# Two feed-forward layers of a diffusion trunk: weight sums and modulation products go to GpSimd

## The chip, the cores and the metric

The kernel runs on one core of one Trainium2 chip. The metric is the device time of one execution in microseconds (us); the engines are TensorE (PE in the profile), VectorE (DVE), ScalarE (ACT), GpSimd (POOL) and SyncE (SP). Each engine runs its own list of instructions in order, and waits on semaphores for the others.

## The reference

The reference is a two-layer diffusion backbone over 256 latent tokens with 256 context tokens before them, width 1024, in float32. Each layer is

```
x = x + mx[2] * 0.5 * swiglu(modulate(x, gain0, mx[0], mx[1]), ffn1_w1, ffn1_w3, ffn1_w2)
x = x + mx[5] * token_mixer(...)
x = x + mx[8] * 0.5 * swiglu(modulate(x, gain2, mx[6], mx[7]), ffn2_w1, ffn2_w3, ffn2_w2)
mx = split(silu(c) @ ada_w[l] + ada_b[l], 9)          # conditioning: 9 vectors of 1024 per layer
swiglu(h, w1, w3, w2) = (silu(h @ w1) * (h @ w3)) @ w2   # hidden width 2816
```

The context tokens go through the same weights with their own conditioning (c_ctx); in layer 1 they drop out after the mixer. The change touches two things in it: how the four feed-forward blocks and the conditioning vectors (one matrix-vector product per layer and stream) are computed.

## The kernel before

Everything is feature-major: a tile holds 128 features by 512 tokens (256 latent, 256 context). A float32 matmul is made of three fp32r ones: each weight tile is loaded raw (512 KB, 128x1024), ScalarE rounds it to a high part (whi), VectorE subtracts that from the raw tile for the low part (wlo), and PE runs wlo, whi, whi against the split activations (lines 216 to 218).

**Stages.** In order of time: start-up and feed-forward 1 of layer 0; the mixer of layer 0; feed-forward 2 of layer 0; feed-forward 1 of layer 1; the mixer of layer 1; feed-forward 2 of layer 1. The two feed-forwards in the middle are the "Strassen" ones (`STRASSEN`): their first half is done by `ff_pairs`, which takes hidden tiles in pairs (pair 1 to 10) and computes the 2x2 block product with 7 block products in place of 8. `product` is one of them: 24 matmuls of 128x256. For a pair, the four raw weight blocks are called W0 to W3, and the seven weights are W0, W1, W2+W3 (n), W0+W2+W3, W0+W2, W3 and W1+W0+W2+W3. In the order of PE a pair p is: W1 ("b21"), W0+n ("n2"), n ("n1"), W0+W2 ("n3"), then already W0 of pair p+1 ("b11"), then W3 ("n4") and the seventh ("b22").

**Sums before.** n and W0+W2 are made by a plain load followed by a second load on GpSimd's queue that adds into the tile (`block(src, plus)`, line 529); W0+n (line 570) and the seventh sum (line 588) are VectorE additions of 128x1024. W0, W2 and W3 are loaded twice or three times a pair: seven loads for four blocks.

**Groups.** After 8, 8 and 6 hidden tiles (`FF_GROUPS`) an out phase multiplies them by w2: for each of 8 output tiles a weight unit and 8 (or 6) times three matmuls of 128x512, and VectorE adds the result to x (line 412).

**Conditioning.** `ada` is a generator: a step loads one 128x1024 block of the conditioning matrix to one of two `araw` buffers (SP queue) and runs one VectorE dot product per stream (`ada_dot`, line 281; the condition vector is spread over all partitions). `hook(n)` pulls steps worth 2n dots after each hidden tile or pair and after each output tile, at the pace in `PACE`. Vectors 2 to 8 of layer 0 and 0 to 2 of layer 1 are made during the first feed-forward, 3 and 4 of layer 1 in the second, 5 to 8 of layer 1 (latent stream only) in the third.

**Order.** PE's list is as the code is written. The lists of all other engines and queues are put in order by a scheduler ahead of time, so an instruction that is written later can stand ahead of one that is written earlier.

Of the kernel before, what the change touches and what calls it, by code (L numbers as in the profile page):

```python
# [20 lines left out]
D = 1024  # L21
KD = 8
# [29 lines left out]
PACE = ((3.2, 1.5), (0.0, 1.0), (0.0, 1.0))  # L52
# [25 lines left out]
class Builder:  # L78
    TAGS = {"sq": ("a", 2, T), "mod": ("a", 2, T), "silu": ("b", 2, T), "th": ("b", 2, T), "on": ("b", 2, T),
            "gg": ("c", 3, T), "PT": ("c", 3, T), "junk": ("c", 3, T), "acc": ("acc", 2, T), "tail": ("b", 2, T), "s1": ("a", 2, T), "sw": ("a", 2, T), "sv": ("kc", 1, T), "su": ("b", 2, T),  # L80
# [203 lines left out]
    def ada(self, l, mods, cond):  # L284
# [3 lines left out]
        for m in mods:  # L288
            ns = (0,) if l == DEPTH - 1 and m > 4 else (0, 1)
            for k in range(KD):  # L290
                raw = self.araw[k % 2]
                nc.sync.dma_start(raw, a["ada"][l, m, k])
                self.ada_dot(l, m, k, raw, cond, ns)
                if k < KD - 1:
                    yield len(ns)
            for s in ns:
                d = M[:, s, m, :]
                nc.vector.tensor_tensor(out=d, in0=d, in1=sm[:, SM_ADAB + m * KD:SM_ADAB + (m + 1) * KD], op=ALU.add)
# [106 lines left out]
    def out_phase(self, getw, acts, l, gm, halves, acc, after, pre, each=None):  # L405
# [13 lines left out]
        nfirst = 2 if gm == 5 or len(halves) == 1 else 0  # L419
# [105 lines left out]
    def block(self, src, plus=None):  # L525
        raw = self.rawp.tile([128, 1024], F32, tag="raw", name="raw")
        self.nc.sync.dma_start(raw, src)
        if plus is not None:
            self.nc.gpsimd.dma_start(raw, plus, accum_op=ALU.add)
# [12 lines left out]
    def ff_pairs(self, l, i, pairs, B):  # L542
# [3 lines left out]
        add = nc.vector.tensor_tensor  # L546
        begun = {}

        def begin(p):
# [5 lines left out]
            begun[p] = r0, q1, s1  # L555

        out = []
        for p in pairs:
            if p not in begun:
                begin(p)  # L560
            r0, q1, s1 = begun.pop(p)
            g1, g2 = (self.pair("g") for _ in range(2))
            r1 = self.block(W[p, 1])
# [19 lines left out]
            r4 = self.block(W[p, 3])  # L583
            self.product(q1, self.cut_weight(r4), B["n4"], False, True)
# [3 lines left out]
            add(out=r1, in0=r1, in1=r0, op=ALU.add)  # L588
# [14 lines left out]
    def ffn(self, l, i, halves, first, acc, after, pre, begun=None, each=None):  # L603
# [22 lines left out]
        for gi, (f0, f1) in enumerate(FF_GROUPS):  # L626
# [16 lines left out]
            w2 = a["w2c"][l, i] if gi == 2 else a["w2a"][l, i, gi]  # L643
            end = gi == len(FF_GROUPS) - 1
# [3 lines left out]
    def startup(self):  # L648
# [82 lines left out]
        self.adaq = itertools.chain(self.ada(0, range(2, NMOD), cond), self.ada(1, range(3), cond))  # L731
# [692 lines left out]
    def build(self):  # L1424
# [8 lines left out]
        for l in range(DEPTH):  # L1433
# [11 lines left out]
            if not last:  # L1445
                self.adaq = self.ada(l + 1, range(3, 5), self.cond(nc.scalar))
# [6 lines left out]
            else:  # L1453
# [3 lines left out]
                self.adaq = self.ada(l + 1, range(5, NMOD), self.cond(nc.scalar))  # L1457
# [58 lines left out]
def _layout(i):  # L1516
# [16 lines left out]
    g["w2c"] = _cols(w2[:, :, 2048:], 128)  # L1533
    w = np.stack([g["w13"][li] for li in STRASSEN])
# [55 lines left out]
```

## Time and profile before

| | |
|---|---|
| median of 3 runs (lowest, highest) | 2303.07 us (2299.65, 2303.67) |
| profiled execution | 2294.51 us, of it span 2292.6 us |
| mean granted PE clock (1 is full speed) | 0.986 |
| busy share of the span | PE 96%, DVE 71%, ACT 46%, POOL 6% |

The span runs from the first to the last instruction, and some 2 us lie around it. Matmuls overlap each other, so the busy share of PE says when it had work, not how fast it went; its waits and its clock in a stage say what the stage lost.

### The profile page before, as it was taken

Reading aid. Unit: us, or ns where it says so; the run is one execution under the profiler, and the core shown is the slowest. Engines: PE = TensorE matmul, PEld = TensorE weight load, DVE = VectorE, ACT = ScalarE, POOL = GpSimd, SP = SyncE. Lnnn points to the kernel's source line nnn. Section 1 sums busy time; section 2 is a strip of 40 time slices with the busy share of each in tenths; the row PEclk is TensorE's granted clock in tenths of the full one; section 3 lists DMA queues with packets and bytes.
Section 4 is the critical chain, followed back from the end, with each engine's and each line's share of the span. In section 5 each row is a group of like instructions: output and inputs, shape, how many; then the busy total and the mean of one; then the engine's idle time right before and its main releaser. Section 6 shows DMA issues by size and latency. Waiting matters only on the chain.

```text
span 2292.6 us, 36217 instructions
## 1 busy us (share of the span) xinstructions
PE 2207.6 (96%) x13578; PEld 1933.6 (84%) x13578; DVE 1621.8 (71%) x3604; ACT 1058.1 (46%) x2617; POOL 131.8 (6%) x166
## 2 busy tenths in 40 slices
PE   9989989999999999999999998989999999999998
PEld 6868777887788877898898998888988889989998
DVE  4899998658645455678875776777567786777665
ACT  4413223437533256444353545335354574565554
POOL 2000000000000000000000000000000000110000
PEclk9999999999999999999999999999999999999999
DMA  8567665331213313436764635885452233435553
GB/s 316 193 220 230 228 209 193 122 101 56 74 54 97 94 61 96 140 93 199 219 174 119 176 79 152 268 248 173 127 176 91 96 111 116 152 117 178 185 184 111
DMA packets 98271, 345.44 MB, mean 151 GB/s; under 512 B 11312, under 2 KB 12208, under 8 KB 98096
## 3 DMA queue, kind: packets, MB, share of 16 engines
q1 hardware_dynamic: 89568, 313.76, 41.6%
q0 software_dynamic: 7808, 27.27, 6.1%
q8 instruction: 107, 1.75, 0.3%
q10 hardware_dynamic: 720, 2.11, 0.3%
q14 instruction: 68, 0.56, 0.1%
HBM read 338.89 MB, written 4.19 MB: 150 GB/s over the span
## 4 chain that ended last, share of the span: by engine, by line
PE 60%; DVE 16%; issue 11%; DMA 11%; ACT 2%; POOL 0%; POOLq 0%; DVEq 0%; SPq 0%; ACTq 0%
PE mm L216 15%; PE mm L217 15%; PE mm L218 14%; DVE junk L281 7%; DMA raw<-in_w13p 5%; DMA araw<-in_ada 5%; DVE wlo L522 2%; DVE wlo L207 2%; PE s L216 2%; PE s L217 2%; PE s L218 2%; PE o L211 2%; PE s L211 2%; PE t L211 2%; PE t L912 1%
## 5 line engine op out<-in xcount | busy, mean ns | idle before, releaser
L206 ACT CAST whi<-raw 128x256 fp32r<-128x256 f32 (+1 forms) x1222 | 437.9, 421 | 391.7 <-PE mm L218 139.1
L207 DVE TENSOR_TENSOR wlo<-raw,whi 128x256 fp32r<-128x256 f32 x1214 | 481.8, 440 | 185.0 <-ACT whi L206 183.1
L216 PE MATMUL mm<-h,wlo 128*128 128x256 f32 (+2 forms) x1272 | 435.4, 342 | 0.4 <-DVE wlo L207 0.4
L218 PE MATMUL mm<-h,whi 128*128 128x256 f32 (+2 forms) x1272 | 426.3, 335 | 0.0
L217 PE MATMUL mm<-h,whi 128*128 128x256 f32 (+2 forms) x1272 | 426.0, 335 | 0.0
L216 PE MATMUL mm<-g,wlo 128*128 128x512 f32 (+1 forms) x758 | 269.5, 355 | 25.0 <-DVE wlo L207 20.1
L281 DVE SCALAR_TENSOR_TENSOR junk<-araw,cond 128x1024 bf16<-128x1024 f32 x224 | 271.6, 1218 | 22.7 <-DMA araw<-in_ada 22.3
L217 PE MATMUL mm<-g,whi 128*128 128x512 f32 (+1 forms) x758 | 266.7, 352 | 3.2 <-DVE g L601 1.7
L216 PEld LDWEIGHTS mm<-h,wlo 128*128 128x128 f32 (+1 forms) x1272 | 241.1, 190 | 33.2 <-issue 9.4
L218 PE MATMUL mm<-g,whi 128*128 128x512 f32 (+1 forms) x758 | 265.9, 351 | 0.0
L218 PEld LDWEIGHTS mm<-h,whi 128*128 128x128 f32 (+1 forms) x1272 | 240.9, 189 | 25.4
L217 PEld LDWEIGHTS mm<-h,whi 128*128 128x128 f32 (+1 forms) x1272 | 241.3, 190 | 22.4 <-issue 0.2
L216 PE MATMUL s<-h,wlo 128*128 128x256 f32 (+1 forms) x848 | 259.0, 305 | 0.0
L217 PE MATMUL s<-h,whi 128*128 128x256 f32 (+1 forms) x848 | 258.6, 305 | 0.0
L218 PE MATMUL s<-h,whi 128*128 128x256 f32 (+1 forms) x848 | 258.5, 305 | 0.0
L521 ACT CAST whi<-raw 128x1024 fp32r<-128x1024 f32 x140 | 145.5, 1047 | 162.3 <-DMA raw<-in_w13p 84.4
L522 DVE TENSOR_TENSOR wlo<-raw,whi 128x1024 fp32r<-128x1024 f32 x140 | 170.1, 1220 | 29.0 <-ACT whi L521 29.0
L216 PEld LDWEIGHTS mm<-g,wlo 128*128 128x128 f32 x758 | 144.1, 190 | 52.0 <-DVE wlo L207 19.9
L216 PE MATMUL mm<-tf,wlo 128*128 128x256 f32 x480 | 144.9, 302 | 35.9 <-DVE wlo L522 28.7
L216 PEld LDWEIGHTS s<-h,wlo 128*128 128x128 f32 x848 | 163.4, 193 | 6.8
L217 PEld LDWEIGHTS s<-h,whi 128*128 128x128 f32 x848 | 163.1, 192 | 6.7
L218 PEld LDWEIGHTS s<-h,whi 128*128 128x128 f32 x848 | 162.9, 192 | 6.7
(296 smaller groups left out, 3851.5 us busy)
## 6 DMA issues: line engine op xcount, KB each, us to landing
araw<-in_ada SPq DMA_DIRECT2D x128, 512.0 KB, 4.1
raw<-in_w13p SPq DMA_DIRECT2D x100, 512.0 KB, 3.5
raw<-in_w SPq DMA_DIRECT2D x90, 512.0 KB, 4.3
raw<-in_win SPq DMA_DIRECT2D x90, 512.0 KB, 3.5
raw<-in_w2a SPq DMA_DIRECT2D x64, 512.0 KB, 4.1
raw<-in_w13p POOLq DMA_DIRECT2D x40, 512.0 KB, 6.1
raw<-in_w2c SPq DMA_DIRECT2D x32, 384.0 KB, 3.1
raw<-in_wbr SPq DMA_DIRECT2D x24, 512.0 KB, 3.5
```

Source lines behind the costliest of these rows:

```text
L206: nc.scalar.copy(hi[:, c], raw[:, c])
L207: eng.tensor_tensor(out=lo[:, c], in0=raw[:, c], in1=hi[:, c].bitcast(F32), op=ALU.subtract)
L211: self.nc.tensor.matmul(out, lhsT=lhsT, rhs=rhs, start=start, stop=stop)
L216: nc.tensor.matmul(out, lhsT=sl, rhs=mh, start=start, stop=False, **kw)
L217: nc.tensor.matmul(out, lhsT=sh, rhs=ml, start=False, stop=False, **kw)
L218: nc.tensor.matmul(out, lhsT=sh, rhs=mh, start=False, stop=stop, **kw)
L281: self.nc.vector.scalar_tensor_tensor(out=junk, in0=raw, scalar=1.0, in1=cond[s], op0=ALU.mult, op1=ALU.mult, accum_out=self.mods[l][:, s, ...
L521: nc.scalar.copy(hi, raw)
L522: nc.vector.tensor_tensor(out=lo, in0=raw, in1=hi.bitcast(F32), op=ALU.subtract)
L912: nc.tensor.transpose(pt[:, b * 128:(b + 1) * 128], P[:, b * 128:(b + 1) * 128], self.ident)
```

## The change

In the two Strassen feed-forwards each weight block is loaded once. All four sums of a pair are GpSimd additions of 128x1024 (`sums`): n when the pair is begun, then n+W0 in place, W2+W0 in place, and W1+n in place. W1 and n live in the pool of activations (`qkv`), the others in the four raw buffers as before.

The conditioning of layer 1 leaves VectorE: a step loads its block on GpSimd's own queue, GpSimd multiplies it by the condition vector in two halves of 128x512 per stream (`ada_product`), and ScalarE adds each half up while copying it in place. Vectors 0 to 3 of layer 1 are made in the second feed-forward, 4 to 8 in the third; the first one keeps only layer 0's seven vectors. `PACE` is changed with it.

Out phases in the two Strassen feed-forwards come after 6, 6, 6 and 4 hidden tiles (`ST_GROUPS`, weights laid out anew in w2s and w2t), that is four in place of three with the same matmuls in all. Where an out phase has 6 hidden tiles, its first two output tiles are now multiplied together, hidden tile by hidden tile (`nfirst`).

```diff
-PACE = ((3.2, 1.5), (0.0, 1.0), (0.0, 1.0))
+PACE = ((2.2, 0.9), (1.5, 0.6), (1.2, 0.6))
+ST_GROUPS = ((0, 6), (6, 12), (12, 18), (18, 22))
...
+    def ada_product(self, l, m, k, raw, cond, streams, part):
+        nc = self.nc
+        for s in streams:
+            for i in range(2):
+                c = slice(i * T, (i + 1) * T)
+                j = self.tmp("prod")
+                nc.gpsimd.tensor_tensor(out=j, in0=raw[:, c], in1=cond[s][:, c], op=ALU.mult)
+                out = part[:, s, k:k + 1] if i else self.mods[l][:, s, m, k:k + 1]
+                nc.scalar.activation(j, j, AF.Copy, accum_out=out)
...
-                nc.sync.dma_start(raw, a["ada"][l, m, k])
-                self.ada_dot(l, m, k, raw, cond, ns)
+                (nc.gpsimd if pool else nc.sync).dma_start(raw, a["ada"][l, m, k])
+                if pool:
+                    self.ada_product(l, m, k, raw, cond, ns, part)
+                else:
+                    self.ada_dot(l, m, k, raw, cond, ns)
...
-        nfirst = 2 if gm == 5 or len(halves) == 1 else 0
+        nfirst = 2 if gm == 5 or len(halves) == 1 or len(acts) == 6 else 0
...
+        sums = nc.gpsimd.tensor_tensor
...
+            r2, r3 = self.block(W[p, 2]), self.block(W[p, 3])
+            n = self.block(None, self.qkv)
+            sums(out=n, in0=r2, in1=r3, op=ALU.add)
+            begun[p] = r0, r2, r3, n, q1, s1
...
-            n = self.block(W[p, 2], W[p, 3])
             wn = self.cut_weight(n)
-            add(out=r0, in0=r0, in1=n, op=ALU.add)
-            self.product(q1, self.cut_weight(r0), B["n2"], False, False)
+            sums(out=n, in0=n, in1=r0, op=ALU.add)
+            self.product(q1, self.cut_weight(n), B["n2"], False, False)
             sv = self.tmp("sv")
             nc.scalar.copy(sv, q1)
+            sums(out=r2, in0=r2, in1=r0, op=ALU.add)
             self.product(q3, wn, B["n1"], True, False)
-            r3 = self.block(W[p, 0], W[p, 2])
-            self.product(q1, self.cut_weight(r3), B["n3"], False, False)
+            sums(out=r1, in0=r1, in1=n, op=ALU.add)
+            self.product(q1, self.cut_weight(r2), B["n3"], False, False)
...
-            r4 = self.block(W[p, 3])
-            self.product(q1, self.cut_weight(r4), B["n4"], False, True)
+            self.product(q1, self.cut_weight(r3), B["n4"], False, True)
...
-            add(out=r1, in0=r1, in1=r0, op=ALU.add)
...
-        self.adaq = itertools.chain(self.ada(0, range(2, NMOD), cond), self.ada(1, range(3), cond))
+        self.adaq = self.ada(0, range(2, NMOD), cond)
...
-                self.adaq = self.ada(l + 1, range(3, 5), self.cond(nc.scalar))
+                self.adaq = self.ada(l + 1, range(4), self.cond(nc.scalar), True)
...
-                self.adaq = self.ada(l + 1, range(5, NMOD), self.cond(nc.scalar))
+                self.adaq = self.ada(l + 1, range(4, NMOD), self.cond(nc.scalar), True)
```

GpSimd's list before, from the reload of x after the mixer of layer 0 to the end of the third feed-forward (line 529 is the adding load, line 333 the power for a norm):

```order
L1388 DMA x<-spill_646 128x512 x8
L529 DMA raw<-in_w13p 128x1024
L333 TENSOR_TENSOR rstd<-ms,neghalf 128x2
L529 DMA raw<-in_w13p 128x1024
L333 TENSOR_TENSOR rstd<-ms,neghalf 128x2
L529 DMA raw<-in_w13p 128x1024 x19
L333 TENSOR_TENSOR rstd<-ms,neghalf 128x2
```

It holds nothing else there: 40 adding loads and the norms.

GpSimd's list in the changed kernel at the same place, from the second sum of pair 1 to the third of pair 2 in the second feed-forward (line 576 is n, 594 is W2+W0, 590 is n+W0, 596 is W1+n; line 290 is a half product, line 303 the load of a conditioning block):

```order
L594 TENSOR_TENSOR raw<-raw 128x1024
L590 TENSOR_TENSOR raw<-raw 128x1024
L596 TENSOR_TENSOR raw<-raw 128x1024
L576 TENSOR_TENSOR raw<-raw 128x1024
L303 DMA araw<-in_ada 128x1024 x2
L594 TENSOR_TENSOR raw<-raw 128x1024
L290 TENSOR_TENSOR prod<-araw,cond 128x512 x4
L303 DMA araw<-in_ada 128x1024
L290 TENSOR_TENSOR prod<-araw,cond 128x512 x4
L303 DMA araw<-in_ada 128x1024
L290 TENSOR_TENSOR prod<-araw,cond 128x512 x4
```

Behind the last of these rows stand a load and then line 590 of pair 2: three conditioning blocks (12 half products) have come to stand between n of pair 2 and n+W0 of pair 2.

The same list at pair 3, up to its line 590 (ahead of these rows, and behind line 594 of pair 3, stand five half products and two loads, then six blocks of four half products and a load each):

```order
L290 TENSOR_TENSOR prod<-araw,cond 128x512 x4
L303 DMA araw<-in_ada 128x1024
L290 TENSOR_TENSOR prod<-araw,cond 128x512 x4
L303 DMA araw<-in_ada 128x1024
L290 TENSOR_TENSOR prod<-araw,cond 128x512 x3
L590 TENSOR_TENSOR raw<-raw 128x1024
L290 TENSOR_TENSOR prod<-araw,cond 128x512
L596 TENSOR_TENSOR raw<-raw 128x1024
```

In all, 40 half products and 10 loads stand between lines 594 and 590 of pair 3, among them products whose hooks are written behind pair 5 and in the second out phase. In the second feed-forward 107 half products, 28 loads and 14 sums stand between n of pair 2 and n+W0 of pair 5 (that included), and the last product of the stage stands ahead of n+W0 of pair 6. In the third feed-forward, where a block has four half products for vector 4 and two for vectors 5 to 8, it is 74 half products, 31 loads and 14 sums to the same place.

VectorE's list before, in the middle of the second feed-forward (line 522 is wlo of a block, 598 and 601 belong to `gated`):

```order
L601 TENSOR_TENSOR g<-sw,g 128x256
L570 TENSOR_TENSOR raw<-raw 128x1024
L522 TENSOR_TENSOR wlo<-raw,whi 128x1024
L588 TENSOR_TENSOR raw<-raw 128x1024
L522 TENSOR_TENSOR wlo<-raw,whi 128x1024
L598 TENSOR_TENSOR su<-su 128x256
L590 TENSOR_TENSOR sv<-sv,s 128x512
L522 TENSOR_TENSOR wlo<-raw,whi 128x1024
```

and in the changed kernel (line 538 is wlo, 617 and 620 are `gated`):

```order
L538 TENSOR_TENSOR wlo<-raw,whi 128x1024 x2
L600 SCALAR_TENSOR_TENSOR sw<-sw,s 128x512
L617 TENSOR_TENSOR sw<-sw 128x256
L620 TENSOR_TENSOR g<-sw,g 128x256
L617 TENSOR_TENSOR su<-su 128x256
L620 TENSOR_TENSOR g<-su,g 128x256
L609 TENSOR_TENSOR sv<-sv,s 128x512
```

The two additions of a pair (570, 588) are gone from it, and no dot (281) stands in this stage's list any more.

## Rows read from the trace of the kernel before

**Rows 1.** Busy time by stage: PE, PEld, DVE, ACT, POOL (instructions), clock, DMA share, GB/s.

```profile
60.00:425.00 365.00, 340.97 (x1522) 277.74 (x1521) 323.31 (x696) 111.03 (x296) 4.86 (x8) 0.99 0.64 212
995.40:1345.00 349.60, 331.74 (x2265) 309.69 (x2265) 251.26 (x429) 162.88 (x303) 17.02 (x20) 0.98 0.60 170
1370.00:1729.00 359.00, 334.10 (x2247) 312.17 (x2246) 251.06 (x424) 160.48 (x299) 19.75 (x26) 0.96 0.63 187
```

**Rows 2.** Groups of VectorE in the first feed-forward, 60 to 425 us.

```profile
L281 DVE SCALAR_TENSOR_TENSOR junk<-araw,cond 128x1024 bf16<-128x1024 f32 x160 | 193.9, 1218 | 9.4 <-DMA araw<-in_ada 9.2
```

**Rows 3.** Groups of VectorE in the second feed-forward, 995.4 to 1345 us.

```profile
L522 DVE TENSOR_TENSOR wlo<-raw,whi 128x1024 fp32r<-128x1024 f32 x68 | 82.5, 1220 | 14.2 <-ACT whi L521 14.2
L281 DVE SCALAR_TENSOR_TENSOR junk<-araw,cond 128x1024 bf16<-128x1024 f32 x32 | 38.7, 1216 | 1.8 <-DMA araw<-in_ada 1.7
L570 DVE TENSOR_TENSOR raw<-raw 128x1024 f32<-128x1024 f32 x9 | 11.0, 1226 | 32.3 <-DMA raw<-in_w13p 32.3
L601 DVE TENSOR_TENSOR g<-sw,g 128x256 fp32r<-128x256 f32 x10 | 4.2, 422 | 3.4 <-ACT g L600 3.4
L598 DVE TENSOR_TENSOR sw<-sw 128x256 f32<-128x256 f32 x10 | 4.2, 418 | 0.0
```

**Rows 4.** Groups of GpSimd in the whole span.

```profile
L529 POOL DMA_DIRECT2D raw<-in_w13p x40 | 34.2, 856 | 690.6 <-DMA raw<-in_w13p 244.0 <-DVE x L412 107.0 <-DVE wlo L522 104.0
L207 POOL TENSOR_TENSOR wlo<-raw,whi 128x768 fp32r<-128x768 f32 x8 | 14.6, 1829 | 21.2 <-ACT whi L206 21.2
L1388 POOL DMA_DIRECT2D x<-spill x16 | 8.8, 550 | 120.2 <-DVE hacc L384 120.2
```

**Rows 5.** GpSimd, one instruction after another: two single-input copies of different width.

```profile
1955.48 0.69 POOL L1220 COPY mqk<-krope 32x512 f32<-32x512 f32 x1
1959.76 0.49 POOL L1220 COPY mqk<-qrope 32x256 f32<-32x256 f32 x1
```

**Rows 6.** Loads over the span: queue, count, KB each, median us from issue to landing.

```profile
raw<-in_w13p SPq DMA_DIRECT2D x100, 512.0 KB, 3.5
raw<-in_w13p POOLq DMA_DIRECT2D x40, 512.0 KB, 6.1
x<-spill POOLq DMA_DIRECT2D x8, 256.0 KB, 3.5
```

**Rows 7.** PE's instructions in time: start us, us, line.

```profile
1001.80 0.28 PE L217 MATMUL mm<-tf,whi 128*128 128x256 f32 x1
1001.92 0.28 PE L218 MATMUL mm<-tf,whi 128*128 128x256 f32 x1
...
1083.70 0.39 PE L218 MATMUL mm<-g,whi 128*128 128x512 f32 x1
1083.93 0.39 PE L216 MATMUL mm<-g,wlo 128*128 128x512 f32 x1
```

**Rows 8.** ScalarE groups, 955 to 1370 us: whi of a block, a 128x512 copy.

```profile
L521 ACT CAST whi<-raw 128x1024 fp32r<-128x1024 f32 x72 | 74.8, 1048 | 78.1 <-DMA raw<-in_w13p 37.6 <-PE mm L218 32.6 <-PE s L218 7.7
L578 ACT COPY sw<-mm 128x512 f32<-128x512 f32 x10 | 5.9, 587 | 15.6 <-PE mm L218 15.6
```

**Rows 9.** VectorE and GpSimd at the same moments: start us, us, line.

```profile
44.62 0.49 DVE L377 SCALAR_TENSOR_TENSOR h<-mod,mods,h 128x256 fp32r<-128x256 f32 x1 [0.19 <-ACT h L376]
45.39 1.82 POOL L207 TENSOR_TENSOR wlo<-raw,whi 128x768 fp32r<-128x768 f32 x1 [3.35 <-ACT whi L206]
45.75 1.74 DVE L377 SCALAR_TENSOR_TENSOR h<-mod,mods,h 128x256 fp32r<-128x256 f32 x1 [0.65 <-ACT h L376]
...
1956.66 3.06 POOL L1220 COPY mqk<-krope 32x512 f32<-32x512 f32 x1
1956.82 2.42 DVE L207 TENSOR_TENSOR wlo<-raw,whi 128x256 fp32r<-128x256 f32 x7
```

More of the change, by code (lines that the diff above doesn't have):

```diff
@@ L1 @@
 import heapq
-import itertools
 import math
@@ L282, in ada_dot, with ada @@
                                                 accum_out=self.mods[l][:, s, m, k:k + 1])
-    def ada(self, l, mods, cond):
+    def ada_product(self, l, m, k, raw, cond, streams, part):
[7 more added lines that the diff above has]
+                nc.scalar.activation(j, j, AF.Copy, accum_out=out)
+    def ada(self, l, mods, cond, pool=False):
         nc, a = self.nc, self.a
@@ L289, in ada @@
             ns = (0,) if l == DEPTH - 1 and m > 4 else (0, 1)
+            part = self.sp.tile([128, 2, KD], F32, tag="part", name="part", bufs=1) if pool else None
             for k in range(KD):
                 raw = self.araw[k % 2]
-                nc.sync.dma_start(raw, a["ada"][l, m, k])
-                self.ada_dot(l, m, k, raw, cond, ns)
+                (nc.gpsimd if pool else nc.sync).dma_start(raw, a["ada"][l, m, k])
[3 more added lines that the diff above has]
+                    self.ada_dot(l, m, k, raw, cond, ns)
                 if k < KD - 1:
@@ L297, in ada @@
                 d = M[:, s, m, :]
+                if pool:
+                    nc.vector.tensor_tensor(out=d, in0=d, in1=part[:, s, :], op=ALU.add)
                 nc.vector.tensor_tensor(out=d, in0=d, in1=sm[:, SM_ADAB + m * KD:SM_ADAB + (m + 1) * KD], op=ALU.add)
@@ L523, in cut_weight, with block @@
         return hi, lo
[L525 to L529, printed above, removed]
+    def block(self, src, pool=None):
+        if pool is None:
+            raw = self.rawp.tile([128, 1024], F32, tag="raw", name="raw")
+        else:
+            raw = pool.tile([128, 1024], F32, tag="pair", name="raw")
+        if src is not None:
+            self.nc.sync.dma_start(raw, src)
         return raw
@@ L554, in begin @@
             nc.scalar.copy(s1, q1)
-            begun[p] = r0, q1, s1
-        out = []
+            r2, r3 = self.block(W[p, 2]), self.block(W[p, 3])
+            n = self.block(None, self.qkv)
+            sums(out=n, in0=r2, in1=r3, op=ALU.add)
+            begun[p] = r0, r2, r3, n, q1, s1
         for p in pairs:
@@ L560, in ff_pairs @@
                 begin(p)
-            r0, q1, s1 = begun.pop(p)
+            r0, r2, r3, n, q1, s1 = begun.pop(p)
             g1, g2 = (self.pair("g") for _ in range(2))
-            r1 = self.block(W[p, 1])
+            r1 = self.block(W[p, 1], self.qkv)
             q2, q3 = self.s_bank(), self.s_bank()
@@ L625, in ffn @@
         h = self.hn
-        for gi, (f0, f1) in enumerate(FF_GROUPS):
+        st = (l, i) in STRASSEN
+        groups = ST_GROUPS if st else FF_GROUPS
+        for gi, (f0, f1) in enumerate(groups):
             gts = start
@@ L642, in ffn @@
             ng = f1 - f0
-            w2 = a["w2c"][l, i] if gi == 2 else a["w2a"][l, i, gi]
-            end = gi == len(FF_GROUPS) - 1
+            end = gi == len(groups) - 1
+            if st:
+                j = STRASSEN.index((l, i))
+                w2 = a["w2t"][j] if end else a["w2s"][j, gi]
+            else:
+                w2 = a["w2c"][l, i] if end else a["w2a"][l, i, gi]
             self.out_phase(lambda c: self.unit(w2[c], ng * 128), gts, l, gm, halves,
@@ L1533, in _layout @@
     g["w2c"] = _cols(w2[:, :, 2048:], 128)
+    w2 = np.stack([w2[li] for li in STRASSEN])
+    g["w2s"] = _cols(w2[:, :2304].reshape(len(STRASSEN), 3, 768, D), 128)
+    g["w2t"] = _cols(w2[:, 2304:], 128)
     w = np.stack([g["w13"][li] for li in STRASSEN])
```

2 lines of the change are left out of this document (1 added, 1 removed).

## The prediction

> **What bounds the kernel now.** I read the busy times by stage first [rows 1]. In each of the three feed-forwards that the change touches, PE is the bound, with little lost: the stage less PE's busy time is 24 us, 18 us and 25 us, and the granted clock of 0.99, 0.98 and 0.96 costs another 4, 7 and 14 us (stage times what is missing to 1). That makes 28, 25 and 39 us, 92 us in all: no change to the other engines can win more here. Next, who is behind these waits. In the first feed-forward VectorE is busy 323 of 365 us, 194 us of it the 160 dots of the conditioning [rows 2]. In the second, VectorE idles 32 us before the addition of line 570 for the adding load of a weight sum [rows 3]; the busy times of the third are alike [rows 1]. GpSimd has next to nothing to do in these stages (17 and 20 us) [rows 1].
>
> **What goes away.** Layer 0's seven vectors need 112 dots, so 48 of the 160 leave the first feed-forward: 48 x 1.22 = 58 us off an engine with 42 us to spare. VectorE then has 265 of 365 us to do and follows PE; I take 24 of the 28 us as won. In each of the other two stages 32 dots (39 us) and some 20 additions (20 x 1.22 = 24 us) leave VectorE, and the second and third loads of a block leave the queues. The added out phase brings 16 additions of 128x256 per stage, at the 0.42 us of such an operation [rows 3] 7 us: they cost nothing as long as the 63 us are gone from VectorE. The paired first output tiles have the same matmuls: nothing.
>
> **What GpSimd gets, and its price.** Before, GpSimd runs one kind of two-operand work on wide tiles: 128x768 in 1.83 us [rows 4]. In proportion, a half product (512) is 1.22 us and a sum (1024) 2.44 us; with a fixed share of 0.3 us, read off two copies of 512 and 256 that take 0.69 and 0.49 us [rows 5], they are 1.32 and 2.34. I take 1.25 and 2.4. A load on GpSimd's queue holds it 0.55 us (reload of x) to 0.86 us (adding load) [rows 4]; I take 0.7. It lands after 3.5 us (256 KB) to 6.1 us (512 KB, adding) [rows 6]; I take 5.
>
> The Trainium skill (GPSIMD Engine Reference, Performance versus the Vector engine) gives 4497 ns for such an addition of 2048 elements, about half VectorE's rate, and advises VectorE for it. An estimate from that page, in proportion, is 1.12 and 2.25 us; by it the lateness worked out next would be about 16 us and 11 us smaller in the two stages. The row of this case stands above it.
>
> **Where the sums come to stand.** What decides is GpSimd's order, not its sum. A block product takes PE 24 x 0.12 = 2.9 us, a pair 20.2 us, an out phase of six 8 x 18 x 0.227 = 32.7 us [rows 7]. Counted from pair 1's first product, PE without a wait comes to n2 of pair 2 at 25.9 us, of pair 3 at 78.8, of pair 4 at 99.0, of pair 5 at 119.1. Each n2 needs n+W0 (line 590) plus its whi and wlo, 1.05 + 1.22 = 2.3 us [rows 3, 8].
>
> On GpSimd, n of pair 2 can be done at about 12 us: W3's buffer is free once W0+W2 of pair 1 is cut (2.9 + 2.3), its load lands 3.5 us later [rows 6], the sum takes 2.4, and semaphores come on top. From there to n+W0 of pair 5 the order has 107 half products (134 us), 14 sums (34 us) and 28 loads (20 us), with some 2 us for the first landing: 190 us. Two buffers hide the other landings, since a block's own work (4 x 1.25 + 0.7 = 5.7 us) is longer than 5. So n2 of pair 5 starts at 12 + 190 + 2.3 = 204 us where 119 was due: **84 us late**. It falls into four waits: 14 us at pair 2, 35 at pair 3 (40 half products stand ahead of its line 590), 18 each at pairs 4 and 5. Then PE has 52.9 us of its own to n2 of pair 6 (six products, an out phase, one product) against 21 half products, four sums and four loads, 39 us: no further wait, and the 84 us stay.
>
> In the third feed-forward it is 74 half products (93 us), 14 sums (34 us), 31 loads (22 us). A one-stream block has only 2 x 1.25 + 0.7 = 3.2 us of work, less than a landing: with two buffers 0.9 us of each of 21 blocks can show, 19 us at most; sums stand among them, I take 10. So 12 + 158 + 2.3 = 172 us for 119: **53 us late**. The rest (22 half products, four sums, nine loads, 43 us) is again under PE's 52.9.
>
> ScalarE gets 128 sums in the second and 96 in the third stage, at the 0.59 us of a 128x512 copy [rows 8] 75 and 56 us on top of 163 and 160: not the bound.
>
> **The two engines against each other.** At 45.75 us a VectorE operation with both inputs in SBUF that otherwise takes 0.49 us takes 1.74 us, until 0.3 us after GpSimd's subtraction ends; at 1956.66 us a GpSimd copy takes 3.06 instead of 0.69 us, through seven VectorE subtractions in a row [rows 9]. So they shut each other out. Such work of VectorE is 7 x 1.22 + 8 x 0.42 = 11.9 us a pair [rows 3], 48 us on the four pairs to n2 of pair 5. Bounds: nothing, where it all falls into GpSimd's load issues and landings (22 and 32 us), or all 48. I take 25 and 15 us. In pairs 6 to 10, with no products left, 4 x 2.4 + 11.9 = 21.5 us stand against PE's 20.2: 1.3 us for some nine pairs, I take 10 (0 to 25).
>
> **The sum.** First feed-forward -24; second 84 + 25, less the 25 us that it loses now, +84; third 53 + 15 - 39 = +29; later pairs +10: +99 us. On the profiled 2294.5 us that is 2394; the median of the runs lies 9 us above the profiled one, so I say 2400.
>
> **Rivals.**
> - *No shutting out to speak of* (22%). GpSimd's products wait for ScalarE to free their buffers, which leaves gaps for VectorE. Then -24 + 59 + 14 + 4 = +53: 2356.
> - *Full shutting out* (16%). Every VectorE operation with two SBUF inputs delays GpSimd by its whole time, as the seven in [rows 9] did: 84 + 48 - 25, 53 + 48 - 39, 25 in the later pairs, less 24: +170, 2473. The Trainium skill (SBUF — State Buffer, Who interferes with whom) states this rule: the read interface is lent for a whole instruction, and the other engine stands still. The rows agree with it for single instructions; none shows two engines that are both busy for long.
> - *GpSimd keeps up, and the kernel gets faster* (9%). The price of a half product decides: 0.1 us of it moves the two stages by 10.7 + 7.4 = 18 us, so from the +53 of the first rival, no loss is left at 1.25 - 0.29 = 0.96 us. At the 0.69 us of the 512-wide copy [rows 5] the stages would be 24 and 13 us late instead of 84 and 53: 53 - 100 = -47, 2256. Against it: that copy has one input, and all eight two-operand rows average 1.83 us for 768 [rows 4].
> - *No change to be told* (3%): a price just at that point.
>
> **How the numbers follow.** The forecast, with half of the shutting out, has 50% (2370 to 2445). A measurement of this kernel tells about 0.2%, 5 us, from no change. Forecast, first and second rival are slower, 88%; faster 9%; same 3%. The range runs from below the first rival (2330) to near the second (2460), and leaves out the faster case and the upper half of the full one.
>
> **What would show it.** In the profile after: GpSimd busy over half of both Strassen stages, 224 half products near 1.25 us and 80 sums near 2.4 us or longer; PE waiting at L216 for wlo of n+W0 (line 538) at pairs 2 to 5, the longest at pair 3 in each stage, and its clock down behind these waits; the second feed-forward near 430 us and the third near 390; VectorE's wlo stretched while GpSimd runs; the first feed-forward with PE's waits under 8 us. The prediction is wrong if half products take under 1 us, if GpSimd's order leaves line 590 on time although they don't, or if ScalarE's sums, and not GpSimd, hold the products up by far more than counted.

## The result and the profile after

The changed kernel takes 2552 us where the kernel before takes 2303: ratio 1.1081 (1.1059 to 1.1103). The direction was right; the loss is 249 us and not the 97 that were forecast, and it lies above the range. To see where it went, I cut both spans at the same landmarks: a stage runs from the first cut of the activation forms (line 493 before, 509 after) to the last addition into x (line 412, 428). First the two stages before, then after (columns as in [rows 1]):

```profile
999.10:1346.70 347.60, 329.74 (x2248) 307.66 (x2247) 249.54 (x430) 160.79 (x301) 17.02 (x20) 0.98 0.61 171
1374.50:1733.60 359.10, 334.20 (x2245) 312.14 (x2245) 251.02 (x430) 158.57 (x300) 20.57 (x27) 0.96 0.64 188
```

```profile
967.40:1478.70 511.30, 371.49 (x2232) 338.55 (x2232) 345.80 (x339) 243.59 (x514) 295.95 (x199) 0.85 0.31 102
1510.40:1982.80 472.40, 357.78 (x2231) 326.76 (x2231) 309.68 (x332) 221.28 (x451) 252.64 (x183) 0.87 0.36 119
```

All that lies ahead of the second feed-forward is 31.7 us shorter (999.1 to 967.4): the first feed-forward is rid of its waits. The second is 163.7 us longer and the third 113.3; between them it is 3.9, behind them 10.2. Of the 277 us of the two stages, 212 are idle time of PE (stage less busy: 17.9 and 24.9 us before, 139.8 and 114.6 after), and 65 are slower matmuls: as many instructions keep PE busy 41.8 and 23.6 us longer, at a granted clock of 0.85 and 0.87 between the levels of 1.2 and 2.4 GHz.

No engine is full. GpSimd's 296 us are not the loss by themselves: what stands out is VectorE, which runs 91 instructions fewer than before in the second stage and is busy 96 us longer. Its groups from 967.4 to 1300 us of the changed kernel (busy time and mean ns behind the bar):

```profile
L538 DVE TENSOR_TENSOR wlo<-raw,whi 128x1024 fp32r<-128x1024 f32 x38 | 67.4, 1792 | 23.7 <-ACT whi L537 23.7
L617 DVE TENSOR_TENSOR sw<-sw 128x256 f32<-128x256 f32 x5 | 25.4, 5082 | 3.6 <-ACT sw L616 3.6
L620 DVE TENSOR_TENSOR g<-sw,g 128x256 fp32r<-128x256 f32 x5 | 13.8, 2757 | 2.4 <-ACT g L619 2.4
L428 DVE SCALAR_TENSOR_TENSOR x<-mm,mods,x 128x256 f32<-128x256 f32 x32 | 13.8, 476 | 4.9 <-PE mm L218 4.9
L600 DVE SCALAR_TENSOR_TENSOR sw<-sw,s 128x512 f32<-128x512 f32 x5 | 3.4, 686 | 7.2 <-ACT sw L599 7.2
```

Against [rows 3]: the split of a block takes 1792 ns for 1220, the product of line 617 takes 5082 for 418. The two groups that take one operand from PSUM, the additions into x and line 600, keep their time. Before, from 999.1 to 1346.7 us, they are:

```profile
L412 DVE SCALAR_TENSOR_TENSOR x<-mm,mods,x 128x256 f32<-128x256 f32 x48 | 21.2, 478 | 30.4 <-PE mm L218 30.3
L579 DVE SCALAR_TENSOR_TENSOR sw<-sw,s 128x512 f32<-128x512 f32 x10 | 6.9, 686 | 6.7 <-ACT sw L578 6.7
```

And GpSimd's half products over the whole span are little longer than the 1.25 us that I took:

```profile
L290 POOL TENSOR_TENSOR prod<-araw,cond 128x512 f32<-128x512 f32 x224 | 309.7, 1406 | 56.4 <-ACT prod L292 39.1
```

So the shutting out (one of the two engines standing still beside the other) falls on VectorE. One place shows how it reaches PE: the timeline of four engines at the end of pair 5 (start us, us; in brackets the wait ahead, and for whom).

```profile
1237.19 4.74 DVE L207 TENSOR_TENSOR wlo<-raw,whi 128x768 fp32r<-128x768 f32 x1
1241.86 6.41 DVE L617 TENSOR_TENSOR sw<-sw 128x256 f32<-128x256 f32 x1
...
1236.11 5.00 POOL L290 TENSOR_TENSOR prod<-araw,cond 128x512 f32<-128x512 f32 x4
...
1242.02 2.42 POOL L576 TENSOR_TENSOR raw<-raw 128x1024 f32<-128x1024 f32 x1
1244.39 1.29 POOL L290 TENSOR_TENSOR prod<-araw,cond 128x512 f32<-128x512 f32 x1
1245.64 2.33 POOL L594 TENSOR_TENSOR raw<-raw 128x1024 f32<-128x1024 f32 x1
...
1248.30 0.41 ACT L619 CAST g<-sw 128x256 fp32r<-128x256 f32 x1 [8.89 <-DVE sw L617]
...
1250.33 0.82 ACT L206 CAST whi<-raw 128x768 fp32r<-128x768 f32 x1
...
1251.17 2.02 DVE L207 TENSOR_TENSOR wlo<-raw,whi 128x768 fp32r<-128x768 f32 x1 [2.01 <-ACT whi L206]
...
1253.34 0.76 PE L216 MATMUL mm<-g,wlo 128*128 128x512 f32 x1 [7.73 <-DVE wlo L207]
```

VectorE's 0.42 us product ends 0.3 us after GpSimd's third instruction in a row (1245.64 + 2.33). ScalarE waits 8.89 us for it, the cast of the next weight unit stands behind in ScalarE's order, then VectorE's split, and PE waits 7.73 us. The largest of PE's waits from 967.4 to 1478.7 us (us, times, longest), 119 of some 140 us, all name a split of VectorE. Not every one was followed back to a held instruction:

```profile
PE s L216 <- DVE wlo L538: 43.4, 4, 12.1
PE mm L216 <- DVE wlo L538: 39.4, 9, 10.9
PE mm L216 <- DVE wlo L207: 36.1, 10, 7.7
```

### The profile page after: what moved, and what is told of

Read it like the earlier page. It is cut to its first block, busy times and chain, and to the rows that moved or that the text cites. A ratio compares the mean times of both kernels' runs of the same rounds, so it can differ in the third digit from the quotient of the medians.

```text
span 2552.0 us, 36430 instructions
## 1 busy us (share of the span) xinstructions
PE 2267.9 (89%) x13542; PEld 1981.3 (78%) x13542; DVE 1719.1 (67%) x3306; ACT 1203.6 (47%) x2985; POOL 648.5 (25%) x502
## 4 chain that ended last, share of the span: by engine, by line
PE 56%; issue 18%; POOL 11%; DVE 7%; DMA 4%; ACT 4%; POOLq 0%; SPq 0%; DVEq 0%; ACTq 0%
PE mm L216 14%; PE mm L217 13%; PE mm L218 13%; POOL prod L290 6%; PE s L216 3%; PE s L217 3%; PE s L218 3%; DVE wlo L538 2%; PE o L211 2%; PE s L211 2%; DMA raw<-in_w2s 2%; POOL raw L590 2%; DMA araw<-in_ada 2%; DVE wlo L207 1%; DVE sw L617 1%
## 5 line engine op out<-in xcount | busy, mean ns | idle before, releaser
L207 DVE TENSOR_TENSOR wlo<-raw,whi 128x256 fp32r<-128x256 f32 (+2 forms) x1134 | 504.5, 489 | 292.8 <-ACT whi L206 290.7
L206 ACT CAST whi<-raw 128x256 fp32r<-128x256 f32 (+2 forms) x1142 | 432.0, 439 | 388.0 <-issue 117.3
L216 PE MATMUL mm<-h,wlo 128*128 128x256 f32 (+2 forms) x1272 | 435.6, 342 | 0.0
L216 PE MATMUL mm<-g,wlo 128*128 128x512 f32 (+1 forms) x746 | 277.1, 371 | 72.0 <-DVE wlo L207 50.9
L216 PE MATMUL s<-h,wlo 128*128 128x256 f32 (+1 forms) x848 | 267.1, 315 | 73.6 <-DVE wlo L538 73.3
L290 POOL TENSOR_TENSOR prod<-araw,cond 128x512 f32<-128x512 f32 x224 | 309.7, 1406 | 56.4 <-ACT prod L292 39.1
L538 DVE TENSOR_TENSOR wlo<-raw,whi 128x1024 fp32r<-128x1024 f32 x140 | 246.3, 1773 | 104.5 <-ACT whi L537 104.5
L217 PE MATMUL mm<-g,whi 128*128 128x512 f32 (+1 forms) x746 | 273.5, 367 | 6.5 <-DVE g L620 6.5
L218 PE MATMUL mm<-g,whi 128*128 128x512 f32 (+1 forms) x746 | 271.7, 364 | 0.0
L216 PEld LDWEIGHTS mm<-h,wlo 128*128 128x128 f32 (+1 forms) x1272 | 241.3, 190 | 32.5 <-issue 9.4
L217 PE MATMUL s<-h,whi 128*128 128x256 f32 (+1 forms) x848 | 265.5, 313 | 0.0
L218 PE MATMUL s<-h,whi 128*128 128x256 f32 (+1 forms) x848 | 265.1, 313 | 0.0
L216 PE MATMUL mm<-tf,wlo 128*128 128x256 f32 x480 | 153.7, 320 | 104.3 <-DVE wlo L538 88.6
L216 PEld LDWEIGHTS s<-h,wlo 128*128 128x128 f32 x848 | 170.3, 201 | 82.2 <-DVE wlo L538 44.7
L216 PEld LDWEIGHTS mm<-g,wlo 128*128 128x128 f32 x746 | 147.1, 197 | 103.3 <-issue 48.3
L216 PEld LDWEIGHTS mm<-tf,wlo 128*128 128x128 f32 x480 | 106.6, 222 | 109.6 <-DVE wlo L538 92.6
L292 ACT ACTIVATE prod<-prod 128x512 f32<-128x512 f32 x224 | 140.6, 628 | 106.7 <-POOL prod L290 99.1
```

Of the source, the lines that this page charges most:

```text
L206: nc.scalar.copy(hi[:, c], raw[:, c])
L207: eng.tensor_tensor(out=lo[:, c], in0=raw[:, c], in1=hi[:, c].bitcast(F32), op=ALU.subtract)
L216: nc.tensor.matmul(out, lhsT=sl, rhs=mh, start=start, stop=False, **kw)
L217: nc.tensor.matmul(out, lhsT=sh, rhs=ml, start=False, stop=False, **kw)
L218: nc.tensor.matmul(out, lhsT=sh, rhs=mh, start=False, stop=stop, **kw)
L290: nc.gpsimd.tensor_tensor(out=j, in0=raw[:, c], in1=cond[s][:, c], op=ALU.mult)
```

## The experiments

My theory at first was the prediction's own, Q: the products queued ahead of line 590 make the lateness. The rival, S: the two engines shut each other out. The first four runs take the change apart. Each run's edit is shown in part; `...` or a bracket stands for the rest.

**e1, the sums alone on GpSimd.**

```diff
-                self.adaq = self.ada(l + 1, range(4), self.cond(nc.scalar), True)
+                self.adaq = self.ada(l + 1, range(4), self.cond(nc.scalar))
```

(and the same in the third stage, vectors 4 to 8)

> The changed kernel, but layer 1's conditioning is done as before, by dots on VectorE with loads on SP's queue, at the new pace; GpSimd keeps the weight sums, and the groups of six stay. Theory Q (the products queued ahead of line 590 made the lateness, and all that followed from it): without products GpSimd has 4 x 2.45 = 9.8 us a pair against PE's 20.2, so both stages return to about their length before (348 and 359 us), the first feed-forward keeps its 28 us: 2265 to 2300. Rival S (the two engines shutting each other out is enough by itself): 9.8 us of GpSimd, 11.9 of VectorE and some 4 of dots make 25.5 us a pair, 5 late on each of 20 pairs: 2350 to 2400.

2408 us, 1.0463 (1.0430 to 1.0496): above S's range even, with no product on GpSimd.

**e2, the products alone on GpSimd.**

```diff
-        sums = nc.gpsimd.tensor_tensor
+        sums = nc.vector.tensor_tensor
```

> The changed kernel, but the four weight sums of a pair are done by VectorE; the products stay on GpSimd. No block waits for GpSimd any more, GpSimd only competes with VectorE for operands. Theory Q: VectorE has about 250 - 39 + 7 + 24 = 242 us to do in 348, so the stages end near their length before: 2270 to 2310. Rival S: the products' 224 x 1.25 us are lost to VectorE's two-operand work, 160 and 120 us in the two stages on 242: 400 and 360 us, 50 us late in the second and little in the third: 2320 to 2360. If the raw buffers held across the out phase and not GpSimd make the lateness, it stays here too: over 2400.

2502 us, 1.0867 (1.0829 to 1.0905). That is far above S's range too, and lies in the range that was set for the raw buffers (e8 prices these). No block waits for GpSimd here, and four fifths of the loss stay. Nothing stands queued ahead of line 590 any more, so Q does not carry it. The place itself shows it, n+W0 of pair 5 in the changed kernel, then in e2:

```profile
1213.06 2.55 POOL L590 TENSOR_TENSOR raw<-raw 128x1024 f32<-128x1024 f32 x1
```
```profile
1204.48 1.21 DVE L590 TENSOR_TENSOR raw<-raw 128x1024 f32<-128x1024 f32 x1
```

Counted from the stage's first cut (967.4 and 964.4 us) it begins at 245.7 us behind GpSimd's queue, and at 240.1 where VectorE makes it.

**e3, GpSimd in program order.**

```diff
-            with tc.manual_schedule(engines={ET.PE}):
+            with tc.manual_schedule(engines={ET.PE, ET.Pool}):
```

(and each block's load issued one block ahead)

> The changed kernel with the same work on every engine, but GpSimd's instructions in the order in which the program writes them (8 to 24 half products between the sums of two pairs, each block loaded one block ahead), in place of the order with 107 half products between n of pair 2 and n+W0 of pair 5. Theory Q: a pair costs GpSimd at most 9.8 + 7.5 + 1.2 = 18.5 us, under PE's 20.2, an out phase 33 for 32.7: 2270 to 2330. Rival S: 18.5 + 11.9 = 30 us a pair, 10 late on each of 16 pairs, and some 7 on each of three out phases: 2430 to 2480, no better by much than the change itself.

2518 us, 1.0935 (1.0903 to 1.0967): above S's range as well. The order is worth 35 us of 249, net of what the new order costs. Q falls. GpSimd now waits itself, in the second stage:

```profile
POOL raw L596 <- DVE wlo L544: 97.7, 10, 20.0
POOL raw L582 <- DMA raw<-in_w13p: 43.9, 9, 5.2
```

**e4, the kernel before with the dots moved.**

```diff
-        self.adaq = itertools.chain(self.ada(0, range(2, NMOD), cond), self.ada(1, range(3), cond))
+        self.adaq = self.ada(0, range(2, NMOD), cond)
-PACE = ((3.2, 1.5), (0.0, 1.0), (0.0, 1.0))
+PACE = ((2.2, 0.9), (1.5, 0.6), (1.2, 0.6))
...
```

(and vectors 0 to 3 in the second stage, 4 to 8 in the third, still as dots)

> The kernel before with one thing of the change alone: the first feed-forward keeps layer 0's seven vectors, layer 1's nine are spread over the second and third at the new pace, all as dots on VectorE with loads on SP's queue. Theory: the first feed-forward gains 28 to 32 us; VectorE goes to about 289 of 348 and 275 of 359 us in the others, so they lose little: 2268 to 2285, a gain of 0.8 to 1.5%. Rival: VectorE at 83% is late for weight splits again and again, as it was in the first feed-forward at 323 of 365 us: each of the two stages loses 10 to 15 us more, and the gain is gone, 2290 to 2305.

2310 us, 1.0036 (1.0022 to 1.0050): the rival, 5 us above its range. The first feed-forward gains 33.4 us (999.1 to 965.7), and the two stages give back 25.7 and 23.5, with VectorE at 77% and 70%:

```profile
965.70:1339.00 373.30, 337.40 (x2248) 312.89 (x2247) 285.65 (x502) 162.00 (x301) 17.02 (x20) 0.95 0.61 182
1366.80:1749.40 382.60, 339.21 (x2246) 316.62 (x2245) 269.71 (x467) 158.90 (x300) 20.57 (x27) 0.93 0.62 187
```

Work on an engine that is not full costs time here, among the pairs as I took it (e12 below does not bear that part out). So I formed a third theory, L: a pair is a loop (load, sum, split, sum, split) through one set of buffers, with little slack against PE's 20.2 us; and a rival B, the raw buffers that a begun pair holds across an out phase.

**e5, the sums on VectorE as well** (e1 with e2's edit).

> The run with the sums alone, but the sums too are done by VectorE: GpSimd has nothing of the change, while the groups of six, the order of the sums and the raw buffers stay. Theory L (a pair is a loop of load, sum, split, sum, split through one set of buffers, and GpSimd's 2.4 to 3.3 us a sum makes it longer than PE's 20.2 us): with 1.22 us a sum the loop is 5 us shorter, and VectorE, at 320 of some 350 us a stage, is late as in the first feed-forward: 2320 to 2350. Rival B (the raw buffers held across an out phase and the extra out phase): nothing of that has changed, so it stays near the 2408 of the sums alone, 2385 to 2415.

2356 us, 1.0239 (1.0211 to 1.0268), just above L's range. So 52 us of e1 come from the sums being on GpSimd.

**e6, the groups of six alone** (e4 with ST_GROUPS and the out phases cut to it).

> The kernel before with the dots moved, and the groups of six tiles besides (two more out phases, w2 cut in rows of six, the first two output tiles of a group begun together); sums and loads as before. It tells what the groups cost by themselves. Theory: 16 additions of 128x256 a stage and no more, 2309 to 2320. Rival B in part: more out phases are more places where loads of weights come late; each of two costs some 8 us, 2325 to 2345.

2324 us, 1.0096 (1.0070 to 1.0122): 14 us, between the two.

**e7, no conditioning of layer 1.**

```diff
-                self.adaq = self.ada(l + 1, range(4), self.cond(nc.scalar), True)
+                nc.vector.memset(self.mods[l + 1], 0.5)
+                nc.vector.memset(self.gs[l + 1], 1.0)
```

> The changed kernel with the conditioning of layer 1 left out altogether (its nine vectors are constants, so neither products, nor loads, nor ScalarE's sums): GpSimd has the 80 sums alone, VectorE no dots. Theory L: a pair's loop by itself is 24 to 26 us, as pairs 7 to 10 of the changed kernel show it with no products left, so some 4 us are lost on each of 20 pairs and 5 on each of four out phases: 2330 to 2375, little less than the sums beside VectorE's dots (2408). Rival S (it is the products and dots beside the sums that made the lateness): no wait is left, 2260 to 2285.

2332 us, 1.0134 (1.0106 to 1.0162), in L's range at its lower end. The sums on GpSimd are bearable as long as nothing else competes. Its stages also show VectorE with only the conditioning gone:

```profile
967.10:1348.10 381.00, 340.03 (x2232) 316.23 (x2232) 248.61 (x317) 158.66 (x256) 102.32 (x39) 0.94 0.27 90
1379.60:1761.40 381.80, 340.28 (x2231) 316.16 (x2232) 250.13 (x315) 158.59 (x259) 105.34 (x47) 0.94 0.28 92
```

In the changed kernel VectorE is busy 97 and 60 us longer than here, with 22 and 17 instructions more, nearly all of them 128x8 wide. But e7 is not VectorE's own work: GpSimd's sums stretch it already. Its splits in the second stage:

```profile
L538 DVE TENSOR_TENSOR wlo<-raw,whi 128x1024 fp32r<-128x1024 f32 x70 | 117.4, 1686 | 48.9 <-ACT whi L537 48.8
```

In e14 below, with next to nothing on GpSimd (0.7 and 5.1 us), they take 1222 ns, and VectorE is busy 246 and 245 us with the 40 sums of a stage (49 us) in it; without them it would be 197 and 196. So GpSimd's sums alone stretch VectorE by some 51 and 54 us a stage in e7, and in the changed kernel the whole stretch is some 145 and 110 us. In e7 the stretch gives back what the sums took off VectorE, and the run is 18 us slower than e14.

**e8, W2 and W3 loaded behind the out phase** (on e1).

```diff
+                if p % 3 != 2:
+                    early = load(p + 1)
...
+            r2, r3, n = early or load(p)
```

> The run with the sums alone (2408), but W2 and W3 of the pair behind an out phase are loaded after that phase's weights, not before them, so three raw buffers and not one are left to the out phase. Rival B: the six out phases that waited for w2s loads (64 us of ScalarE's waits in the second stage) run at PE's pace: 30 to 40 us won, 2365 to 2380. Theory L: the phase is faster, but the pair behind it starts its loop from nothing and gives that back: 2395 to 2420.

2378 us, 1.0341 (1.0309 to 1.0373): B is right for 30 us on e1. The line of ScalarE's waits in the second stage of e1, which has no counterpart among the largest of e8:

```profile
ACT whi L206 <- DMA raw<-in_w2s: 64.5, 20, 5.3
```

The other 144 us, from e1 to the changed kernel, are the products on GpSimd and ScalarE's sums of them. The next runs part these two; all but e16 have the weight sums on VectorE, as e2.

**e10, sums without products; e9, products without sums.**

```diff
-                nc.gpsimd.tensor_tensor(out=j, in0=raw[:, c], in1=cond[s][:, c], op=ALU.mult)
-                nc.scalar.activation(j, j, AF.Copy, accum_out=out)
+                nc.scalar.activation(j, raw[:, c], AF.Copy, accum_out=out)
```

(this is e10; e9 keeps the product and leaves out ScalarE's sum, with constants for the vectors)

> The other half of the same pair: ScalarE keeps its 224 sums, over the loaded block as it is, and GpSimd's products are left out (the nine vectors are then not the reference's). Theory S: with no GpSimd beside it VectorE is back at its own times, and ScalarE has 240 of some 380 us: 2310 to 2350. Rival A: ScalarE's own 64 to 75 us a stage in an engine that issues in order are what costs, 2400 to 2480.

2357 us, 1.0242 (1.0216 to 1.0267): S, or a little over it. VectorE's splits of 128x1024 take 1.22 us again. ScalarE's sums wait for the loaded blocks here, 34.8 us in 36 pieces.

> The run with the products alone (2502; the weight sums are VectorE's), with ScalarE's 224 sums of the products left out (the nine vectors are constants): GpSimd multiplies and nobody waits for it. Theory S (GpSimd's products shut VectorE out of its operands; in that run its splits of 128x1024 took 1.79 us in place of 1.22 and its busy time in the second stage was some 100 us over that work's own): the stages stay long, 2450 to 2500. Rival A (ScalarE, which issues in order, stands at a sum until GpSimd's product is done, 42 us in 56 waits in the second stage, and the casts behind it come late): the time falls to that of the run with all of it on VectorE or below, 2310 to 2360.

2484 us, 1.0796 (1.0769 to 1.0823), far from rival A. But the trace spoils the verdict: a reload of the conditioning vector on ScalarE's queue waits for the last product and holds ScalarE for 93.8 us at one go.

**e13 to e16** were to mend this.

> The run with products and without ScalarE's sums once more, but the conditioning vector is reloaded at the first product of the third feed-forward and not at the end of the second, so that no load on ScalarE's queue waits for GpSimd. Theory S: VectorE is held out as before and only the one hold of 94 us goes: 2380 to 2400. If the hold had hidden other lateness: 2420 to 2480.

2488 us, 1.0811 (1.0795 to 1.0827), above both ranges: the reload was issued as early as before, and the hold is 92.1 us.

> The base of the others: weight sums on VectorE, layer 1's conditioning left out altogether. VectorE has 241 us to do in some 350: 2300 to 2330, a little under the same with GpSimd's sums (2332).

2314 us, 1.0060 (1.0043 to 1.0077), as expected.

> The run with the products alone (2502): GpSimd makes the same products and ScalarE as many sums of the same width, but it sums the loaded block and not the product (the nine vectors are not the reference's), so neither waits for the other. Theory C (what costs most is the chain ScalarE's cast behind a sum behind a product that VectorE holds up): only the shutting out and ScalarE's own time are left, 2395 to 2440. Rival: the two loads as such cost, coupled or not: 2480 to 2510.

> The changed kernel with that one coupling taken away in the same manner; sums and products stay on GpSimd, in its own order. Theory C: 2440 to 2490 in place of 2552. Rival: 2530 to 2560.

2528 us, 1.0987 (1.0970 to 1.1003), and 2569 us, 1.1163 (1.1145 to 1.1180): more than with the real products and above all four ranges. They did not uncouple anything: ScalarE's sums wait for the loaded block instead (143 us in e15), and GpSimd issues those loads behind its products. Inconclusive.

**e17, products that nobody waits for; e18, ScalarE's sums over the conditioning vector.**

```diff
+                kept = self.cond(nc.scalar)
...
-                self.adaq = self.ada(l + 1, range(4, NMOD), self.cond(nc.scalar), True)
+                self.adaq = self.ada(l + 1, range(4, NMOD), kept, True)
```

(both; e17 leaves out ScalarE's sums as e9 does, e18 takes them over `cond` in place of the product)

> Weight sums on VectorE, products on GpSimd, ScalarE's sums left out (the nine vectors are constants), and the conditioning vector loaded once for both stages: no engine waits for GpSimd. What is left against the base of 2314 is the shutting out alone. Theory C (shutting out is the smaller part, waits for GpSimd in ScalarE's queue the larger): 2365 to 2400, the 92 us of the hold gone. Theory S: 2440 to 2490.

> The same with ScalarE's 224 sums of the same width put back, over the conditioning vector (the nine vectors are not the reference's), so they wait for nothing. Against the 2502 of the real products this has the same work on every engine without ScalarE's waits for GpSimd. Theory C: 2390 to 2440. Theory S: 2470 to 2510.

2473 us, 1.0759 (1.0743 to 1.0775), and 2477 us, 1.0763 (1.0744 to 1.0783): both in S's ranges by their totals. But e18 does not price ScalarE's sums. They wait for nothing, so the scheduler put them early: 83 of the 224 run ahead of the second feed-forward, and none in the third:

```profile
L292 ACT ACTIVATE aj<-cond x224: 612/631/634, 868.7 to 1184.0; 128x512 bf16<-128x512 f32 x112
```

And both runs still have one hold in the second stage: VectorE's sum n (line 574 in e17) writes a buffer that the last product must have read (52 us in e18; e17's waits of VectorE):

```profile
DVE raw L574 <- POOL prod L290: 65.9, 1, 65.9
```

Their third stages have none (PE's longest wait there is 12.6 us), so the third stages are what to compare: e14 (neither), e10 (ScalarE's sums), e17 (GpSimd's products), e18 (the same, since no sum of ScalarE is left in it), e2 (both, with their waits):

```profile
1370.10:1745.40 375.30, 338.08 (x2236) 315.39 (x2236) 244.91 (x355) 158.96 (x261) 5.10 (x9) 0.94 0.28 94
```
```profile
1383.00:1787.80 404.80, 347.31 (x2236) 320.96 (x2235) 247.75 (x372) 218.05 (x453) 26.21 (x49) 0.93 0.41 139
```
```profile
1479.70:1902.80 423.10, 350.14 (x2236) 322.10 (x2235) 303.07 (x355) 159.11 (x261) 178.01 (x145) 0.91 0.39 133
```
```profile
1483.60:1911.00 427.40, 348.88 (x2237) 321.09 (x2236) 309.52 (x356) 159.54 (x263) 179.13 (x145) 0.91 0.39 132
```
```profile
1482.10:1932.70 450.60, 360.54 (x2235) 330.58 (x2234) 305.59 (x371) 221.64 (x453) 168.40 (x145) 0.89 0.37 125
```

Products alone +48 us (e18 +52), ScalarE's sums +30, both +75: nearly the sum of the two. Each has something else in it: ScalarE waits 24.8 us for loaded blocks in e10 and 45.7 us for products in e2, and all but e14 load the conditioning blocks (ScalarE's waits for w2s are 77.6 us in e17 for 67.1 in e14). The products run nothing on VectorE, and its busy time rises from 245 to 303 us with the same 355 instructions. That is the shutting out in VectorE's time; what it costs is the 48 us, less what the loads may have in them, which no run parts. In the second stage it is e14 378, e10 389, e17 485 less a PE wait of 68.7 that ends the hold, some 416, and e2 488: products +39, sums +11, and 60 us more when the sums wait for real products (in e2 ScalarE waits for line 290 42 us in 56 pieces there). That last 60, the largest of the three, is a difference; no run shows it by itself.

**e11 and e12, one vector moved in the kernel before.**

```diff
-        ... self.ada(1, range(3), cond))
+        ... self.ada(1, range(2), cond))
...
-PACE = ((3.2, 1.5), (0.0, 1.0), (0.0, 1.0))
+PACE = ((2.9, 1.35), (0.0, 1.5), (0.0, 1.0))
```

(e12: 0.8, 1.0 in the second stage; both make vectors 2 to 4 there)

> The kernel before, with one vector (16 dots) moved from the first feed-forward to the second, where all 48 dots stand in the two out phases that have hooks and none among the pairs. Theory (dots cost where they stand among a pair's products, 64 and 48 dots among pairs having made the two stages 26 and 24 us longer; an out phase has room): the first feed-forward wins some 10 us, the second loses 2 to 5: 2294 to 2300. Rival (VectorE then has 1.22 + 0.96 + 3 x 1.22 = 5.8 us for an output tile that takes PE 5.4, so the out phases are late): 2302 to 2308.

> The same vector moved, but 16 of the 48 dots stand among the pairs, about 1.6 for each, and 32 in the out phases as before. If dots among the pairs are what costs, the 16 cost some 0.6 us each, 10 us, and nothing is won: 2300 to 2308. If not, as much is won as in the run before or more: 2292 to 2298.

0.9963 (0.9949 to 0.9978) and 0.9969 (0.9953 to 0.9986): both a little faster than the kernel before, 2294 and 2293 us. e11 has the gain and the loss that were expected: 11.9 us won ahead of the second feed-forward (987.2 for 999.1), and that stage 357.9 for 347.6 us, 10 lost, more than the 2 to 5; its profiled span is thus no shorter by more than 0.6 us, and the interval of the timed runs is what says faster. In e12 it is 14.5 us won (984.6) and 14.1 lost (361.7). Where the dots stand makes no difference that shows, so e11's theory, that dots among the pairs are what costs, is not borne out.

## Why the prediction was wrong

**What fell.** The step "What decides is GpSimd's order, not its sum". The order is as written there, but putting it right wins 35 us (e3), and with no sum on GpSimd at all 2502 of 2552 us stay (e2). In size the lateness at pair 5 of the second stage is not far off: n+W0 begins at 245.7 us of the stage where e14, without conditioning, has it at 141.7, 104 us late for 84 and 25 of shutting out. That is luck: with nothing queued ahead of it, e2 is as late there (240.1). With products that nobody waits for it is 173.0 (e17), with ScalarE's sums over loaded blocks 154.9 (e10); the rest shows in e2, where ScalarE's sums wait for the products as well. So what carries GpSimd's work to PE is, as far as the runs show it, not the queue ahead of line 590 but VectorE's held instructions and ScalarE's list.

**The term that failed with it.** Shutting out was added to GpSimd's queue, 25 and 15 us, as VectorE's work that delays GpSimd. It is mostly the other way round: GpSimd's half products lose 0.16 us each (1.41 for 1.25), 36 us in all, and VectorE loses some 145 and 110 us, 51 and 54 of them to the sums by themselves (e7). VectorE is followed by ScalarE and PE in a pair's loop, where a late split can be a wait; e17 prices the products' part at some 39 and 48 us, loads included, with no other engine's work waiting for GpSimd but for the one hold. The rival of full shutting out had the right engine pair and the wrong victim, and at 2473 was still 79 us short.

**Costed at nothing.** ScalarE was "not the bound" at 75 and 56 us of sums; it is busy 85 and 63 us longer than in e7. The sums cost 43 us in time (e14 to e10), their waits for the loads included, for ScalarE's casts stand behind them in order, and in the second stage up to 60 more when they wait for products. The groups of six cost 14 us (e6). The raw buffers held across an out phase, which the prediction does not have, cost 30 (e8, on e1). PE's clock behind the waits was named, but left out of the sum: 65 us of slower matmuls. And "no further wait, the 84 us stay" failed behind pair 5: GpSimd waited 35.5 us for a split at pair 6, and in the out phase ahead of it ScalarE waited 2.1 to 6.6 us for each of five w2s loads.

**What held.** The first feed-forward: -24 was said, -31.7 came (no wait of PE left from 60 to 400 us). The prices on GpSimd: 1.25 us was right for a half product by itself, the sums took 2.43 to 2.79 for 2.4. PE's waits stood at L216 for line 538's wlo, as said, at pairs 2 to 5; but at n2 itself they are 10.9, 6.4, 4.0 and 3.1 us where 14, 35, 18 and 18 were said. At pairs 4 and 5 the longest stands one product ahead of n2 (at pair 5 11.9 us at 1209.8 us for the split of W1, a block without a sum), and the waits did not end at pair 5.

**The account.** By medians, one edit at a time: 2302 before; dots moved 2310 (e4); groups 2324 (e6); sums on VectorE with the six buffers in place of the adding load 2356 (e5); sums on GpSimd 2408 (e1); products on GpSimd, summed on ScalarE 2552. These are prices in this order: the step of the sums to GpSimd costs 52 us beside the dots, and 18 without any conditioning (e14 to e7). Of the 10 us behind the third feed-forward 6 come with the groups (e4 559.0 us there as before, e6 565.0); the other 4 are not explained.

## What to carry to other kernels

Before work goes to GpSimd because it is idle, ask which VectorE operations with both inputs in SBUF lie on the path to PE: each of GpSimd's instructions can hold them for its length and more, and what is freed on VectorE by count is given back in stretched time (e7: 49 us freed a stage, 51 and 54 given back). In a loop through few buffers, price a move by the loop's slack and not by engine totals: here VectorE at 70 to 77% passed most of the added time on. In an experiment that takes a wait away, look in the trace for the next hold of the same kind, and for where the scheduler now puts the freed instructions, before reading the total.

## What the runs showed of the hardware

How VectorE and GpSimd share is not the same everywhere. In the changed kernel a 0.42 us product stood through three GpSimd instructions in a row, 6.41 us. In the rows of e17 here VectorE gets its turn after each of GpSimd's products (its timeline, start us, us, then GpSimd's):

```profile
995.07 2.32 DVE L574 TENSOR_TENSOR raw<-raw 128x1024 f32<-128x1024 f32 x1
997.31 1.51 DVE L618 TENSOR_TENSOR g<-sw,g 128x256 fp32r<-128x256 f32 x1
998.74 2.31 DVE L592 TENSOR_TENSOR raw<-raw 128x1024 f32<-128x1024 f32 x1
1000.98 1.49 DVE L615 TENSOR_TENSOR su<-su 128x256 f32<-128x256 f32 x1
...
1006.01 0.68 DVE L607 TENSOR_TENSOR sv<-sv,s 128x512 f32<-128x512 f32 x1
...
994.76 14.69 POOL L290 TENSOR_TENSOR prod<-araw,cond 128x512 f32<-128x512 f32 x8 [2.79 <-DMA araw<-in_ada]
```

1.21 us become 2.3 and 0.41 become 1.5, 1.1 us each, a little under one half product; eight products take 14.7 us for 10.0. Line 607, with one operand in PSUM, keeps its 0.68 us. The Trainium skill (SBUF — State Buffer, Who interferes with whom) says that outside the modes with two ports a VectorE instruction with at most one SBUF input does not contend with GpSimd, that one with two inputs in SBUF does, and that the shared pair of ports is an exclusive lock; these rows agree, and the 6.41 us show that VectorE can stand still through three instructions of GpSimd. A long hold does not need the sums. In e2 GpSimd has products only, and a split of 1.22 us stands through four of them (VectorE, then GpSimd):

```profile
1198.07 6.16 DVE L538 TENSOR_TENSOR wlo<-raw,whi 128x1024 fp32r<-128x1024 f32 x1
...
1198.18 4.96 POOL L290 TENSOR_TENSOR prod<-araw,cond 128x512 f32<-128x512 f32 x4
```

What decides between turns and a long hold was not tried.
